# First layer: half of the out-projection woven into latent attention, three modulation vectors moved to neighbourhood attention

## The chip, the core and the metric

The kernel runs on one core of a Trainium2 chip. TensorE (PE) multiplies, VectorE (DVE) and ScalarE (ACT) do the elementwise work, GpSimd (POOL) has small tasks and a DMA queue of its own, and SyncE (SP) issues nearly all DMAs. The metric is device time in microseconds of one launch, the median of 3 runs; lower is better.

## The reference, cut to what matters

Two layers of a diffusion trunk over 512 latent tokens and 256 context tokens of width 1024. Each layer makes six modulation vectors for each of two streams, three parallel heads, one out-projection over their concatenation, and an MLP:

```python
mx, mc = _modulation(c, w_mod[i], b_mod[i]), _modulation(c_ctx[None], w_mod[i], b_mod[i])  # silu(cond) @ w + b, split in 6
px = _adaln(x, g_norm1[i], mx[0], mx[1]) @ w_in[i]                 # the same for context: pc
o_na  = _na_latent(...)      # 2-D neighbourhood attention, 4 heads of 64
o_mla = _mla_latent(...)     # latent attention, 8 heads
o_hy  = _hyena(...)          # order-2 Hyena, 256 channels
mix = concatenate([o_hy, merge(o_na), merge(o_mla)]) @ w_out[i]    # rows: 256 + 256 + 512
x = x + mx[2] * mix
x = x + mx[5] * _sqrelu_mlp(_adaln(x, g_norm2[i], mx[3], mx[4]), ...)
```

In the last layer only the latent stream is carried on (512 columns); in the first layer both streams are (768).

## The kernel before, in words

All activations lie feature-major: a tile is 128 features by 768 tokens (512 latent, 256 context). Most products run as three float32r matmuls on high and low parts (`wblock` loads 512 KB of weights, ACT makes the high part, DVE the low part). A product over 768 columns is a pair of matmuls of 512 and 256 columns.

One layer runs in this order: input projections; neighbourhood attention (`na_attend`) woven with the Hyena convolution (`hyena`, the name `conv`); latent attention (`mla_attend`); out-projection; MLP. `weave` takes generators with rates and steps each of them by its rate once a round, so the rates set the order in which work is traced. The framework lays out each engine's program from that order when the kernel is built; where nothing pins it, it may put an instruction ahead of one traced earlier if its inputs and a buffer are there (the first three blocks of `w_out` are loaded long before the out-projection is traced).

**Neighbourhood attention, first layer.** `na_attend` makes 16 rounds: in a round it scores unit u, writes the output of unit u-4 and transposes unit u-2; 8 units are latent, 4 context only. `hyena` has 14 steps at rate 1.4: 4 transposes, then for each of two orders two forward transforms (16 PE instructions each, then eight DVE operations that make `z`), and inverse transforms that need all of `z`. PSUM has 2 double banks ("mm") and 4 single banks ("b") here. The three buffers of the tag `raw` serve all weight blocks.

**Latent attention, first layer.** `mla_attend` makes 52 rounds for 48 units, in four groups of 12: 8 units over all 768 keys and then 4 that see 256 context keys only. In the first two of those four rounds the next two heads are turned (`heads_in`, 12 transposes a head). PSUM is 3 mm and 2 b banks. Woven into it at rate 0.2 each are `modulation` for vectors 2 and 4 (loads by SP; 32 matmuls of 32 x 256 a vector, which run four at a time in column groups) and `modulation_rows` for vector 3 (loads by SP, two DVE multiply-and-reduce operations for each of 8 blocks, and a SiLU over `cond_rows`).

**Out-projection.** In the last layer, `out_first` weaves the first half (contraction blocks 0 to 3: Hyena and neighbourhood outputs `mh`, `ml`) into latent attention, adds it to the residual `xT` through the gate, and only blocks 4 to 7 follow. In the first layer all 8 blocks follow latent attention: 8 output blocks x 8 contraction blocks x 3 x (512, 256) matmuls at L1341, while `fill` steps `modulation_rows` for (0,5) and the six vectors of layer 1 (L191) on DVE, one step an output block. `fill` goes on in the MLP.

Of the kernel before, what the change touches and what calls it, by code (L numbers as in the profile page):

```python
# [16 lines left out]
ALU = mybir.AluOpType  # L17
# [6 lines left out]
DEPTH = 2  # L24
# [17 lines left out]
def kernel(ctx, tc, A, dbg=None, stop=None):  # L42
    nc = tc.nc
    pe, act, dve, pool, sp = nc.tensor, nc.scalar, nc.vector, nc.gpsimd, nc.sync

# [93 lines left out]

    def mod_weights(l, v, k, p, bufs):  # L140
        w = p([128, 1024], tag="wm", bufs=bufs)
        sp.dma_start(w, A["w_mod"][l, k * 128:(k + 1) * 128, v * 1024:(v + 1) * 1024])
# [147 lines left out]
    H1 = 0.3  # L290
    OF = 1.0
    NSB, NPT = 3, 4
# [741 lines left out]

    def out_weights(j, half):

        return wblock(A["w_outh"][j, half])

    def out_first(l, xT, mh, ml, streams):

        for j in range(4):
            w = out_weights(j, 0)
            for e in range(2):
                t = b_tile()
                for k in range(4):
                    ws, xs = [x[:, e * 512 + k * 128:e * 512 + (k + 1) * 128] for x in w], [x[:, k] for x in (mh, ml)]
                    for i, (wx, mx) in enumerate(((0, 0), (0, 1), (1, 0))):
                        for a, b in streams:
                            pe.matmul(t[:, a:b], ws[wx], xs[mx][:, a:b], start=(k == 0 and i == 0),  # L1049
                                      stop=(k == 3 and i == 2))  # L1050
                    if k % 2:
                        yield
                add_gated(t, xT, 2 * j + e, l, 2, streams)
                yield

    def mlp(l, xT, hh, hl, rstd, streams, p, tail, fill=iter(())):
# [10 lines left out]
        def ff1(c):  # L1067
# [3 lines left out]
            for j in range(4):  # L1071
# [125 lines left out]
    for l in range(DEPTH):  # L1197
# [14 lines left out]
        if l:  # L1212
            squares, sums = mla_in(l, uh, ul, cqh, cql, ssq, sc, fill, late)
            sc.close()
            gp.close()
            xp.close()
# [63 lines left out]
        if not last:  # L1280
            hyena_out(1, y, mh, ml)
        weave((na_attend(l, na, nb, mh, ml, sc), 1.0), (conv, (1.4, 1.4)[l]))
        hyena_out(0, y, mh, ml)
        sc.close()
        hs.close()
        bp.close()
        yp.close()
# [9 lines left out]
        psum_banks(3)  # L1297
        if last:
            xp = Pool(f"x{l + 1}", "right")
            xT, acc = xp([128, KD, nt]), xp([128, nt])  # L1300
            sp.dma_start(xT, xd)
            weave((mla_attend(l, qrs, qk0, qkd[l], vd[l], mh2, ml2, sc), 1.0),
                  (out_first(l, xT, mh, ml, streams), OF))
        else:
            wmp = Pool("wm_rest")
            weave((mla_attend(l, qrs, qk0, qkd[l], vd[l], mh2, ml2, sc), 1.0),
                  (chain(*[modulation(0, v, wmp) for v in (2, 4)]), 0.2),
                  (modulation_rows([(0, 3)], cond_rows(wmp), wmp), 0.2))
            wmp.close()
        sc.close()  # L1310
# [4 lines left out]

        if not last:
            xp = Pool(f"x{l + 1}", "right")
            xT, acc = xp([128, KD, nt]), xp([128, nt])
            sp.dma_start(xT, A["xT"])
        gp = Pool(f"g{l}", "right")  # L1320
# [5 lines left out]
        for m in range(KD):  # L1326
            ks = range(8)
            if last:
# [4 lines left out]
            else:  # L1333
                w = wblock(A["w_out"][l, m])
            t = mm_tile()
# [12 lines left out]
            sumsq(acc, xT, m, nt, xp)  # L1348
            next(fill, None)
        split(hh[:, :, nt:nt + 2], hl[:, :, nt:nt + 2], mods[:, l, 3])  # L1350
# [10 lines left out]
        else:  # L1361
            def tail(m):
                sp.dma_start(xd[:, m], xT[:, m, 0:S])
                sumsq(acc, xT, m, nt, xp)
# [74 lines left out]
def _layout(inp):  # L1439
# [64 lines left out]
    a["w_in_v"] = blocks(np.concatenate([w[:, :, 1280:1536], w[:, :, 1920:]], 2), 8, 288)[:, 0, 0]  # L1504
    a["w_out"] = blocks(g["w_out"][:DEPTH - 1], 8, 128)[:, :, 0]
    a["w_outh"] = g["w_out"][-1].reshape(2, 4, 128, 4, 2, 128).transpose(3, 0, 2, 4, 1, 5).reshape(4, 2, 128, 8, 128)
    a["w_ff1"] = blocks(g["w_ff1"], 8, 128)[:, :, 0]
# [25 lines left out]
```

## Time and profile before

| | us |
|---|---|
| median of 3 runs | 1818.92 (1817.44 to 1821.12) |
| the profiled execution | 1826.58 |
| its span, first to last instruction | 1824.7 |
| neighbourhood attention, first layer | 282.86 to 355.45 |
| latent attention, first layer | 355.45 to 504.01 |
| out-projection, first layer | 504.01 to 571.90 |
| latent attention, last layer | 1324.23 to 1440.51 |

The stage bounds are the starts of the first PE instruction that belongs to the next stage; a few instructions lie across a bound. An fp32 product appears as two PE instructions at the same line, an fp32 transpose or a float32r product as one. A PE instruction's duration includes the time to run through the array, in which the next one already enters; so what a row of them costs is read from starts, not durations. The granted TensorE clock is 1.00 at 2.4 GHz and 0.50 at 1.2 GHz; a value between is a mean over a stretch.

### The profile page before, as it was taken

The numbers are of one execution on the slowest core, as the hardware profiler recorded it, in microseconds if no ns is written. First come the engines' busy times: TensorE is split into PE (matmuls) and PEld (weight loads), VectorE is DVE, ScalarE is ACT, GpSimd is POOL, SyncE is SP. The second block draws the span as 40 slices with busy tenths as digits, with TensorE's granted clock in tenths as the row PEclk, the third lists the DMA queues.
The fourth block names the chain that finished last, engine by engine and source line by source line (L and its number), as shares of the span: only waits on it lengthen the run. The fifth ranks groups of instructions, "written<-read, shape, count | busy, mean of one in ns | idle before, by whom it ended". The sixth has DMA issues, their size and how long they took to land.

```text
span 1824.7 us, 26988 instructions
## 1 busy us (share of the span) xinstructions
PE 1750.7 (96%) x10794; PEld 1498.3 (82%) x10794; DVE 1226.0 (67%) x2247; ACT 754.5 (41%) x1262; POOL 89.6 (5%) x137
## 2 busy tenths in 40 slices
PE   5999988988999999999999999989999999999999
PEld 2788977766688888888888888879787799999997
DVE  5857777877668868677675457686887665555554
ACT  3624326756634413212222225645666653333331
POOL 1134200000000000000000000230000000000000
PEclk9999989999999999999999999899999999999999
DMA  9225423262243433333332122353041023332232
GB/s 345 69 74 169 137 96 119 100 214 96 72 182 108 149 126 116 138 116 122 132 116 70 58 73 90 109 195 118 24 171 45 33 89 96 96 93 93 93 93 81
DMA packets 73388, 206.11 MB, mean 113 GB/s; under 512 B 12556, under 2 KB 24605, under 8 KB 71856
## 3 DMA queue, kind: packets, MB, share of 16 engines
q1 hardware_dynamic: 71664, 199.15, 32.3%
q0 software_dynamic: 1600, 5.24, 0.8%
q8 instruction: 85, 1.39, 0.3%
q14 instruction: 39, 0.32, 0.1%
HBM read 182.35 MB, written 21.23 MB: 112 GB/s over the span
## 4 chain that ended last, share of the span: by engine, by line
PE 86%; DVE 6%; ACT 4%; DMA 2%; issue 2%; POOL 0%; SPq 0%; DVEq 0%; ACTq 0%; POOLq 0%
PE mm L273 54%; PE mm L1341 5%; PE b L1008 3%; PE mm L995 3%; PE mm L131 2%; PE mm L133 2%; PE mm L132 2%; PE b L387 2%; PE b L131 1%; PE b L150 1%; PE b L132 1%; PE b L133 1%; PE b L350 1%; PE b L1049 1%; PE b L758 1%
## 5 line engine op out<-in xcount | busy, mean ns | idle before, releaser
L273 PE MATMUL mm<-t,wh 128*128 128x512 f32 (+1 forms) x2496 | 493.8, 318 | 2.5 <-DVE t L1032 1.3
L136 ACT ACTIVATE wh<-wr 128x1024 fp32r<-128x1024 f32 (+2 forms) x176 | 185.2, 1053 | 592.2 <-PE mm L273 532.3
L273 PEld LDWEIGHTS mm<-t,wh 128*128 128x128 f32 x2496 | 371.9, 189 | 39.4 <-issue 1.9
L273 PE MATMUL mm<-t,wl 128*128 128x512 f32 (+1 forms) x1248 | 297.1, 316 | 0.0
L137 DVE TENSOR_TENSOR wl<-wr,wh 128x1024 fp32r<-128x1024 f32 (+2 forms) x176 | 213.9, 1216 | 30.7 <-ACT wh L136 27.4
L273 PE MATMUL mm<-al,wh 128*128 128x512 f32 (+1 forms) x768 | 233.7, 359 | 0.0
L273 PE MATMUL mm<-ah,wl 128*128 128x512 f32 (+1 forms) x768 | 232.3, 356 | 0.0
L273 PE MATMUL mm<-ah,wh 128*128 128x512 f32 (+1 forms) x768 | 231.0, 355 | 0.0
L1032 DVE SCALAR_TENSOR_TENSOR t<-mm,mods,t 128x512 f32<-128x512 f32 x216 | 136.3, 659 | 140.4 <-PE mm L273 133.4
L273 PEld LDWEIGHTS mm<-t,wl 128*128 128x128 f32 x1248 | 193.7, 189 | 16.0 <-DVE wl L137 0.2
L273 PEld LDWEIGHTS mm<-ah,wl 128*128 128x128 f32 x768 | 127.7, 188 | 22.4
L273 PEld LDWEIGHTS mm<-ah,wh 128*128 128x128 f32 x768 | 126.9, 188 | 23.4
L273 PEld LDWEIGHTS mm<-al,wh 128*128 128x128 f32 x768 | 126.3, 188 | 20.0
L191 DVE SCALAR_TENSOR_TENSOR wmp<-wm,t 128x1024 f32<-128x1024 f32 x64 | 78.4, 1225 | 70.7 <-DMA wm<-in_w_modr_dram 70.7
L425 DVE TENSOR_REDUCE mmx<-mm 128x1 f32<-128x768 f32 (+1 forms) x80 | 67.5, 846 | 25.2 <-PE mm L133 24.5
L136 ACT ACTIVATE ah<-relu 128x768 fp32r<-128x768 f32 (+1 forms) x64 | 47.3, 739 | 86.9 <-DVE relu L1095 86.8
L430 ACT ACTIVATE msb<-mm,mmx,qrs 128x768 f32<-128x768 f32 (+1 forms) x80 | 72.1, 902 | 25.0 <-DVE mmx L427 21.3
L1085 DVE TENSOR_SCALAR bb<-mm,cols 128x2 f32<-128x2 f32 x64 | 14.0, 219 | 97.2 <-PE mm L273 97.0
L996 ACT ACTIVATE mpt<-mm 128x768 f32<-128x768 f32 (+1 forms) x80 | 57.5, 724 | 50.7 <-PE mm L995 50.6
L191 DVE SCALAR_TENSOR_TENSOR wm<-wm,t 128x1024 f32<-128x1024 f32 x64 | 78.1, 1220 | 0.2
L137 DVE TENSOR_TENSOR al<-relu,ah 128x768 fp32r<-128x768 f32 (+1 forms) x64 | 52.6, 823 | 36.2 <-ACT ah L136 36.1
L1341 PE MATMUL mm<-t,wh 128*128 128x512 f32 x320 | 75.2, 348 | 0.0
(294 smaller groups left out, 2864.6 us busy)
## 6 DMA issues: line engine op xcount, KB each, us to landing
wr<-in_w_ff_dram SPq DMA_DIRECT2D x128, 512.0 KB, 3.5
wm<-in_w_modr_dram SPq DMA_DIRECT2D x64, 512.0 KB, 4.4
wm<-in_w_mod_dram SPq DMA_DIRECT2D x32, 512.0 KB, 8.2
wr<-in_w_in_t_dram SPq DMA_DIRECT2D x18, 512.0 KB, 4.4
qk<-qk_spill SPq DMA_DIRECT2D x9, 576.0 KB, 5.2
qk_spill<-upk SPq DMA_DIRECT2D x12, 384.0 KB, 3.0
kx<-kk POOLq DMA_DIRECT2D x16, 256.0 KB, 2.4
wr<-in_w_in_qk_dram SPq DMA_DIRECT2D x8, 512.0 KB, 4.5
```

Of the source, the lines that this page charges most:

```text
L131: pe.matmul(out, sh, mh, start=start, stop=False)
L132: pe.matmul(out, sh, ml, start=False, stop=False)
L133: pe.matmul(out, sl, mh, start=False, stop=stop)
L136: act.activation(hi, src, AF.Copy)
L137: dve.tensor_sub(lo, src, r32(hi))
L191: dve.scalar_tensor_tensor(w if s else junk, w, 1.0, cr[:, s], ALU.mult, ALU.mult, accum_out=mods[:, l, v, k, s:s + 1])
L273: pe.matmul(out_[:, po:po + b - a], wk[wx], mk[mx][:, a:b], start=(k == 0 and i == 0), stop=(k == nk - 1 and i == 2))
L425: dve.tensor_reduce(mx, src, AX.X, ALU.max, negate=True)
L430: act.activation(sb[:, h, :n], src[:, h, :n], AF.Exp, bias=mx[:, h:h + 1], scale=1.0 if scale is None else scale[:, h:h + 1], accum_out=sm ...
L996: act.activation(pt[:, 0:nkt, qt * 128:(qt + 1) * 128], tt[:, :nkt * 128].rearrange("p (c q) -> p c q", q=128), AF.Copy)
L1032: dve.scalar_tensor_tensor(xT[:, m, a:b], t[:, a:b], mods[:, l, v, m, s:s + 1], xT[:, m, a:b], ALU.mult, ALU.add)
L1341: pe.matmul(t[:, a:b], ws[wx], half[mx][:, k % 4, a:b], start=(k == ks[0] and i == 0), stop=(k == 7 and i == 2))
```

## The change

In the first layer only (the last layer's code is rewritten but issues the same work):

- `out_first` is woven into `mla_attend` at rate 0.62 (32 steps), one b bank and one product a stream (512, then 256 columns). `xT` (3 MB) is loaded at the start of latent attention instead of its end. The loop after it keeps blocks 4 to 7.
- Vectors 2, 3 and 4 are made by `modulation` in the neighbourhood stage at rate 1.0: 5 steps a vector, 4 with a group of eight matmuls, one that copies, transposes and adds. The 24 loads of 512 KB are issued by POOL, in turn into `raw` buffers (3) and a new pool `wm_mid` (2 buffers).
- While that weave is traced, PE's order is pinned around the modulation's matmuls: each group of eight comes behind every PE instruction traced before it and ahead of all traced after it.
- `modulation_rows` for vector 3, its SiLU and its 16 DVE operations leave latent attention. The eight `fill` steps of the out-projection go: four now run in the first part of the MLP, four in its last.

```diff
+        def issue(self, r):
+            ins = r.ins
+            if self.on:
+                for prev in self.since if self.inside else []:
+                    self.after(ins, prev)
+                if self.last is not None:
+                    self.after(ins, self.last)
+                if self.inside:
+                    self.since, self.last = [], ins
+                else:
+                    self.since.append(ins)
+            return r
...
     def modulation(l, v, p, bufs=3, ws=None):
-        out = b_tile()
+        out, wk = b_tile(), []
         for k in range(KD):
-            w = ws[k] if ws else mod_weights(l, v, k, p, bufs)
-            for j in range(4):
-                pe.matmul(out[32 * j:32 * j + 32, 0:256], cst[:, k, :], w[:, j * 256:(j + 1) * 256],
-                          start=(k == 0), stop=(k == KD - 1), tile_position=(0, 32 * j))
+            if ws:
+                wk.append(ws[k])
+            elif k % 2:
+                wk.append(mod_weights(l, v, k, p, bufs, pool))
+            else:
+                wk.append(raw_tile())
+                pool.dma_start(wk[k], A["w_mod"][l, k * 128:(k + 1) * 128, v * 1024:(v + 1) * 1024])
             if k % 2:
+                with pe:
+                    for i in (k - 1, k):
+                        for j in range(4):
+                            pe.matmul(out[32 * j:32 * j + 32, 0:256], cst[:, i, :], wk[i][:, j * 256:(j + 1) * 256],
+                                      start=(i == 0), stop=(i == KD - 1), tile_position=(0, 32 * j))
                 yield
...
-    OF = 1.0
+    OF = 0.62
...
     def out_first(l, xT, mh, ml, streams):
         for j in range(4):
-            w = out_weights(j, 0)
+            w = out_weights(l, j, 0)
             for e in range(2):
-                t = b_tile()
-                for k in range(4):
...
+                for s, a, b in STREAM[:len(streams)]:
+                    t = b_tile()
+                    for k in range(4):
+                        ws = [x[:, e * 512 + k * 128:e * 512 + (k + 1) * 128] for x in w]
+                        for i, (wx, mx) in enumerate(((0, 0), (0, 1), (1, 0))):
+                            pe.matmul(t[:, 0:b - a], ws[wx], (mh, ml)[mx][:, k, a:b], start=(k == 0 and i == 0),
                                       stop=(k == 3 and i == 2))
+                        if k % 2 and s == 0:
+                            yield
+                    m = 2 * j + e
+                    dve.scalar_tensor_tensor(xT[:, m, a:b], t[:, 0:b - a], mods[:, l, 2, m, s:s + 1], xT[:, m, a:b],
+                                             ALU.mult, ALU.add)
+                    yield
...
-                for _ in range(FR if c else 0):
+                for _ in range(FR):
                     next(fill, None)
...
+        if not last:
+            wmp = Pool("wm_mid", "right")
+            mid = chain(*[modulation(0, v, wmp, 2) for v in (2, 3, 4)])
...
+            pe.order(True)
+            weave((na_attend(l, na, nb, mh, ml, sc), 1.0), (conv, 1.4),
+                  (mid, 1.0))
+            pe.order(False)
...
+        xp = Pool(f"x{l + 1}", "right")
+        xT = xp([128, KD, nt])
+        sp.dma_start(xT, xd if last else A["xT"])
+        weave((mla_attend(l, qrs, qk0, qkd[l], vd[l], mh2, ml2, sc), 1.0),
+              (out_first(l, xT, mh, ml, streams), (OF, 1.0)[l]))
...
         for m in range(KD):
-            ks = range(8)
-            if last:
-                ks = range(4, 8)
-                if m % 2 == 0:
-                    w2 = out_weights(m // 2, 1)
-                w = [x[:, m % 2 * 512:] for x in w2]
-            else:
-                w = wblock(A["w_out"][l, m])
+            ks = range(4, 8)
+            if m % 2 == 0:
+                w2 = out_weights(l, m // 2, 1)
+            w = [x[:, m % 2 * 512:] for x in w2]
...
-            next(fill, None)
```

## Rows read from the trace of the kernel before

**Rows 1.** The page: busy time of each engine, and the chain by engine.
```profile
PE 1750.7 (96%) x10794; PEld 1498.3 (82%) x10794; DVE 1226.0 (67%) x2247; ACT 754.5 (41%) x1262; POOL 89.6 (5%) x137
PE 86%; DVE 6%; ACT 4%; DMA 2%; issue 2%; POOL 0%; SPq 0%; DVEq 0%; ACTq 0%; POOLq 0%
```
**Rows 2.** Busy time by stage; length, engines with instruction counts, clock, DMA.
```profile
core 0: us, PE busy (x) PEld busy (x) DVE busy (x) ACT busy (x) POOL busy (x), PEclk, DMA share, GB/s
282.86:355.45 72.59, 64.67 (x505) 52.16 (x504) 59.70 (x125) 52.09 (x132) 0.00 (x0) 0.98 0.31 105
355.45:504.01 148.56, 134.92 (x911) 94.47 (x911) 108.94 (x261) 96.09 (x179) 0.00 (x0) 0.97 0.40 138
504.01:571.90 67.89, 67.89 (x392) 59.35 (x391) 52.90 (x85) 24.18 (x33) 0.00 (x0) 1.00 0.46 163
1324.23:1440.51 116.28, 116.26 (x753) 90.94 (x751) 83.57 (x167) 75.93 (x126) 0.00 (x0) 1.00 0.23 83
```
**Rows 3.** PE in order of time, latent attention of the last layer: start, length, line.
```profile
1374.88 0.82 PE L995 MATMUL mm<-ident,msb 128*128 128x128 f32 x6
1375.63 1.08 PE L1008 MATMUL b<-mpt,t 128*64 128x256 f32 x6
...
1377.44 0.29 PE L131 MATMUL mm<-kh,qh 96*128 96x256 f32 x1
1377.56 0.28 PE L132 MATMUL mm<-kl,qh 96*128 96x256 f32 x1
...
1377.89 2.37 PE L1008 MATMUL b<-mpt,t 128*64 128x256 f32 x18
1380.19 0.87 PE L995 MATMUL mm<-ident,msb 128*128 128x128 f32 x6
```
**Rows 4.** PE in order of time, the modulation's matmuls at the start.
```profile
44.49 3.23 PE L150 MATMUL b<-wm,cst 128*32 128x256 f32 x56
```
**Rows 5.** Groups of latent attention, first layer: count, busy us, mean ns, idle before.
```profile
L1008 PE MATMUL b<-mpt,t 128*64 128x256 f32 x218 | 36.1, 392 | 0.6 <-ACT mpt L996 0.5
L995 PE MATMUL mm<-ident,msb 128*128 128x128 f32 x224 | 35.6, 291 | 9.8 <-ACT msb L430 3.9 <-DVE msb L438 2.4 <-DVE ql L959 1.9
L191 DVE SCALAR_TENSOR_TENSOR wmp<-wm,t 128x1024 f32<-128x1024 f32 x8 | 9.8, 1220 | 4.0 <-DMA wm<-in_w_modr_dram 4.0
L171 ACT ACTIVATE t<-t 128x2048 f32<-128x2048 f32 x1 | 1.9, 1914 | 0.0
```
**Rows 6.** Stretches of latent attention, first layer, columns as in the second group.
```profile
401.00:425.79 24.79, 22.00 (x135) 14.60 (x133) 18.37 (x44) 14.02 (x29) 0.00 (x0) 1.00 0.41 135
425.79:440.75 14.96, 12.42 (x82) 9.19 (x80) 10.45 (x28) 8.65 (x17) 0.00 (x0) 0.89 0.34 114
440.75:461.51 20.76, 20.76 (x140) 14.75 (x140) 14.64 (x38) 14.78 (x29) 0.00 (x0) 1.00 0.17 52
```
**Rows 7.** Stretches of neighbourhood attention, first layer, columns as in the second group.
```profile
282.86:300.00 17.14, 11.76 (x93) 9.88 (x93) 12.50 (x33) 15.04 (x38) 0.00 (x0) 0.90 0.78 251
300.00:320.00 20.00, 17.55 (x145) 13.94 (x145) 19.26 (x32) 13.31 (x32) 0.00 (x0) 1.00 0.15 53
```
**Rows 8.** Groups of neighbourhood attention, first layer: two of the DVE operations behind `z`.
```profile
L744 DVE TENSOR_TENSOR tax<-usx,kkx 128x1024 f32<-128x1024 f32 x4 | 4.9, 1220 | 0.0
L746 DVE TENSOR_TENSOR tax<-tax 128x512 f32<-128x512 f32 x4 | 2.8, 688 | 0.0
```
**Rows 9.** DMAs: SP's loads at L142, then POOL's stores at L396.
```profile
DMA to landing us min/median/max: 3.4/8.2/12.3
L396 POOL DMA_DIRECT2D kx<-kk x16: 539/542/710, 72.9 to 154.1; - x16
DMA to landing us min/median/max: 2.3/2.5/3.0
```
**Rows 10.** Out-projection, first layer: the DVE groups of L191.
```profile
L191 DVE SCALAR_TENSOR_TENSOR wmp<-wm,t 128x1024 f32<-128x1024 f32 x11 | 13.5, 1225 | 0.6 <-DMA wm<-in_w_modr_dram 0.6
L191 DVE SCALAR_TENSOR_TENSOR wm<-wm,t 128x1024 f32<-128x1024 f32 x10 | 12.2, 1225 | 0.1
```

More of the change, by code (lines that the diff above doesn't have):

```diff
@@ L43, with __init__, after, matmul @@
     nc = tc.nc
-    pe, act, dve, pool, sp = nc.tensor, nc.scalar, nc.vector, nc.gpsimd, nc.sync
+    act, dve, pool, sp = nc.scalar, nc.vector, nc.gpsimd, nc.sync
+    class Ordered:
+        def __init__(self):
+            self.on, self.inside, self.last, self.since = False, False, None, []
+        def after(self, ins, prev):
+            tc.add_manual_dep(ins, prev.name, mybir.DependencyInfo(
+                mybir.DependencyClass.NoSync, mybir.DependencyReason.DATA))
+        def issue(self, r):
[10 more added lines that the diff above has]
+            return r
+        def matmul(self, *a, **k):
+            return self.issue(nc.tensor.matmul(*a, **k))
+        def transpose(self, *a, **k):
+            return self.issue(nc.tensor.transpose(*a, **k))
+        def order(self, on):
+            self.on, self.last, self.since = on, None, []
+        def __enter__(self):
+            self.inside = True
+        def __exit__(self, *_):
+            self.inside = False
+    pe = Ordered()
     class Stop(Exception):
@@ L137, in split, with mod_weights @@
         dve.tensor_sub(lo, src, r32(hi))
-    def mod_weights(l, v, k, p, bufs):
+    def mod_weights(l, v, k, p, bufs, queue=sp):
         w = p([128, 1024], tag="wm", bufs=bufs)
-        sp.dma_start(w, A["w_mod"][l, k * 128:(k + 1) * 128, v * 1024:(v + 1) * 1024])
+        queue.dma_start(w, A["w_mod"][l, k * 128:(k + 1) * 128, v * 1024:(v + 1) * 1024])
         return w
     def modulation(l, v, p, bufs=3, ws=None):
-        out = b_tile()
+        out, wk = b_tile(), []
         for k in range(KD):
-            w = ws[k] if ws else mod_weights(l, v, k, p, bufs)
-            for j in range(4):
-                pe.matmul(out[32 * j:32 * j + 32, 0:256], cst[:, k, :], w[:, j * 256:(j + 1) * 256],
-                          start=(k == 0), stop=(k == KD - 1), tile_position=(0, 32 * j))
-            if k % 2:
+            if ws:
[5 more added lines that the diff above has]
+                pool.dma_start(wk[k], A["w_mod"][l, k * 128:(k + 1) * 128, v * 1024:(v + 1) * 1024])
+            if k % 2:
+                with pe:
[3 more added lines that the diff above has]
+                                      start=(i == 0), stop=(i == KD - 1), tile_position=(0, 32 * j))
                 yield
@@ L1033, in add_gated, with out_weights @@
                                      ALU.mult, ALU.add)
-    def out_weights(j, half):
-        return wblock(A["w_outh"][j, half])
+    def out_weights(l, j, half):
+        return wblock(A["w_outh"][l, j, half])
     def out_first(l, xT, mh, ml, streams):
         for j in range(4):
-            w = out_weights(j, 0)
+            w = out_weights(l, j, 0)
             for e in range(2):
-                t = b_tile()
-                for k in range(4):
[L1046 to L1049, printed above, removed]
-                                      stop=(k == 3 and i == 2))
[L1051 to L1054, printed above, removed]
+                for s, a, b in STREAM[:len(streams)]:
[4 more added lines that the diff above has]
+                            pe.matmul(t[:, 0:b - a], ws[wx], (mh, ml)[mx][:, k, a:b], start=(k == 0 and i == 0),
+                                      stop=(k == 3 and i == 2))
+                        if k % 2 and s == 0:
[4 more added lines that the diff above has]
+                    yield
     def mlp(l, xT, hh, hl, rstd, streams, p, tail, fill=iter(())):
@@ L1215 @@
             gp.close()
+            ap_.close()
             xp.close()
@@ L1281 @@
             hyena_out(1, y, mh, ml)
-        weave((na_attend(l, na, nb, mh, ml, sc), 1.0), (conv, (1.4, 1.4)[l]))
+        if last:
+            weave((na_attend(l, na, nb, mh, ml, sc), 1.0), (conv, 1.4))
+        else:
+            pe.order(True)
+            weave((na_attend(l, na, nb, mh, ml, sc), 1.0), (conv, 1.4),
+                  (mid, 1.0))
+            pe.order(False)
         hyena_out(0, y, mh, ml)
@@ L1285 @@
         hs.close()
+        if not last:
+            wmp.close()
         bp.close()
@@ L1297 @@
         psum_banks(3)
-        if last:
[L1299 to L1303, printed above, removed]
-        else:
[L1305 to L1309, printed above, removed]
+        xp = Pool(f"x{l + 1}", "right")
[3 more added lines that the diff above has]
+              (out_first(l, xT, mh, ml, streams), (OF, 1.0)[l]))
         sc.close()
@@ L1314 @@
             return finish_all()
[L1316 to L1319, printed above, removed]
+        ap_ = Pool(f"acc{l + 1}", "right")
+        acc = ap_([128, nt])
         gp = Pool(f"g{l}", "right")
@@ L1326 @@
         for m in range(KD):
-            ks = range(8)
-            if last:
-                ks = range(4, 8)
-                if m % 2 == 0:
-                    w2 = out_weights(m // 2, 1)
-                w = [x[:, m % 2 * 512:] for x in w2]
-            else:
-                w = wblock(A["w_out"][l, m])
+            ks = range(4, 8)
+            if m % 2 == 0:
+                w2 = out_weights(l, m // 2, 1)
+            w = [x[:, m % 2 * 512:] for x in w2]
             t = mm_tile()
@@ L1363, in tail @@
                 sp.dma_start(xd[:, m], xT[:, m, 0:S])
-                sumsq(acc, xT, m, nt, xp)
+                sumsq(acc, xT, m, nt, ap_)
                 for s, a, b, o in ((0, 0, S, 0), (1, S, NT, S + 2)):
@@ L1504, in _layout @@
     a["w_in_v"] = blocks(np.concatenate([w[:, :, 1280:1536], w[:, :, 1920:]], 2), 8, 288)[:, 0, 0]
-    a["w_out"] = blocks(g["w_out"][:DEPTH - 1], 8, 128)[:, :, 0]
-    a["w_outh"] = g["w_out"][-1].reshape(2, 4, 128, 4, 2, 128).transpose(3, 0, 2, 4, 1, 5).reshape(4, 2, 128, 8, 128)
+    a["w_outh"] = g["w_out"].reshape(DEPTH, 2, 4, 128, 4, 2, 128).transpose(0, 4, 1, 3, 5, 2, 6).reshape(
+        DEPTH, 4, 2, 128, 8, 128)
     a["w_ff1"] = blocks(g["w_ff1"], 8, 128)[:, :, 0]
```

2 lines of the change are left out of this document (1 added, 1 removed).

## Prediction

> **What bounds the kernel now.** I read the page's totals first, then its chain, then a table of busy time by stage, and only then single groups. The totals and the chain say PE: 96% busy, 86% of the chain [rows 1]. That average hides three stages with different limits [rows 2]. The first layer's out-projection is PE alone: busy for all of its 67.89 us, and DVE and ACT have time left. Latent attention before it shows PE busy for 134.92 of 148.56 us, neighbourhood attention for 64.67 of 72.59 us.
>
> A busy PE is not yet a full one: a single matmul counts as busy while it runs through the array, though another could have entered. So I count instructions and price them by the distance of starts where PE is dense [rows 3]: six transposes of L995 take 0.75 us, 0.125 each; eighteen instructions of L1008 take 2.30 us, 0.128 each; a float32r matmul of 256 columns 0.12 us. In the out-projection 384 matmuls, 192 pairs, fill 67.89 us less eight strays of 0.128: 0.348 a pair, so 0.228 for the 512 columns [rows 2, 3]. The modulation's instructions cost 3.23/56 = 0.058 each [rows 4].
>
> The first layer's latent attention by these prices: 224 x 0.125 + 218 x 0.128 [rows 5], by the code 96 x 0.228 and 144 x 0.12 for scores and 96 x 0.125 to turn heads: 28.0 + 27.9 + 21.9 + 17.3 + 12.0 = 107 us. The two modulation vectors add 128 instructions x 0.058 = 7.4. So 114.5 of 148.56 us are PE's work, and 34 us are gaps, seen or covered. The last layer is the measure of the method: 192 x 0.125 + 192 x 0.128 + 96 x 0.228 + 96 x 0.12 + 80 x 0.125, and 96 x 0.228 for the half out-projection already woven there: 114 of 116.28 us, 98% full at clock 1.00 [rows 2]. The same weave therefore can fill PE.
>
> The Trainium skill (Trainium Kernel Development and Optimization, Performance Expectations) says that matmul busy time is a bad measure because matmuls are pipelined. Rows 2 agree: 134.92 us busy against 114.5 us counted. By the busy column the 33.4 us that move would find 13.6 us of room in latent attention; that is the second rival below.
>
> **Out-projection.** It loses half of its 192 pairs: 96 x 0.348 = **-33.4 us**. What was beside it: DVE was busy 52.90 us, of which the 21 operations of L191 that ran there took 13.5 + 12.2 [rows 2, 10]; they leave. Some 27 us at most remain, less four of eight weight splits, in a stage of 33.5 us. DVE thus stays under PE, by a smaller margin. The second half needs blocks 4 to 7, of which the last comes from the end of latent attention; the last layer starts in the same way with no PE gap. The weights are the same bytes. I bound this term by -34 and -30 (some gaps where DVE is late). The eight `fill` steps go to the MLP's first and last parts, where the other parts already carry four such steps; I price them at nothing, and at up to 1 us if DVE is late at the seam.
>
> **Latent attention.** Added: 96 pairs, 33.4 us of PE, four weight splits, 16 gated adds. Removed: 7.4 us of modulation matmuls, sixteen L191 operations of 1.22 us on DVE, and the SiLU of 1.9 us [rows 5]. That SiLU sits with two table loads in front of the first softmax; the 3.9 us wait of L995 on ACT [rows 5] goes with it. PE's work becomes 107 + 33.4 = 140.4 us. Lower bound of the stage: as full as the last layer, 140.4/0.98 = 143, so -5.5. Upper bound: the stretches over all keys are dense already once DVE is rid of L191 (20.76 us in the third group, 24.79 in the second) [rows 6], so there the woven work costs its full price; only the context stretches (14.96 us with PE busy 12.42, at clock 0.89) [rows 6] can hide it. They are 16 of 52 rounds and take 16 x 0.62 = 10 of the 32 steps, 10.4 us. Then 33.4 - 10.4 = 23 is paid; 3.9 (SiLU), 4 + 4 (the first two groups without L191) and two thirds of 7.4 come off: +6. A PE that no longer idles would also keep its clock: 0.89 over 14.96 us is a loss of 1.6 us. The mean of the ends is about 0; I take **-1 us**, as the last layer speaks for the lower end. The load of `xT` moves here from the end of the stage and lies ahead of the values (1.5 MB) on SP's queue; the first gated add comes in round 5, some 14 us in, and the last layer runs the same order.
>
> **Neighbourhood attention.** Added: 3 x 64 instructions x 0.058 = 11.1 us, and six transposes of 0.12, together 11.8 us of PE; ACT gets three small copies, DVE a few operations on a handful of columns. PE idles for 5.4 us until 300 and for 2.5 us until 320 [rows 7], 7.9 in the stage [rows 2]. The twelve groups lie over the first 14 of 16 rounds, and a round is 72.6/16 = 4.5 us, so seven or eight fall into these two stretches, 0.93 us each: I let them fill the second gap, 2.45 us, and 2.9 of the first, together 5.3. In the second DVE is busy 19.26 of 20 us: there it sets the pace and PE's extra work is free. That gives 11.8 - 5.3 = **+6.5 us**. The lower bound is 0 (all fits beside DVE). The upper: nothing fits, +11.8, and the pinned order adds stalls. A group stands behind everything traced before it; in the round of the second forward transform that is also the inverse transform, which waits for `z`: two operations of 1.22, two of 0.68 and four of 0.69 on DVE, 6.6 us [rows 8]. Today PE goes on with attention meanwhile. There are two such places, so +13 at most: +25 in all. Each falls on a round whose modulation step has no group, so PE has two rounds of attention to fill it with; I charge none of it in the value. The running sum holds one b bank of four for four rounds; this too lies within the upper end.
>
> The loads: 24 x 512 KB through POOL's queue, whose engine is otherwise idle here (0.00 busy) [rows 2]. Five buffers hold two and a half groups, so a load has about two rounds, 9 us, from its buffer's release to its use. SP's loads of this same size took 8.2 us in the median and 3.4 to 12.3; POOL's stores of 256 KB are issued in 0.54 us and land in 2.5 [rows 9]. Five blocks fit into the buffers ahead of the stage; the other 19, 10 MB, add 137 GB/s over 72.6 us to the 105 there now: 242, about the 251 that the first stretch already reaches [rows 2, 7]. I price the loads at nothing beyond the 6.5; what waits behind a late one is all of PE, by the pinned order.
>
> The Trainium skill (SBUF — State Buffer, SBUF: two separate sides) says that GpSimd cannot write the descriptors of its DMAs while DVE runs a two-port operation. No run here shows it: the stores above ran before this stage. By that rule each load would land later by up to one such operation; it raises the chance of the last rival a little.
>
> **Sum.** -33.4 - 1 + 6.5 = -28 us. Against the profiled execution, 1826.58 - 28 = 1798.6; that execution stands 7.7 us above the median shown, so the predicted median is 1818.92 - 28 = **1791**.
>
> **Rivals.** *All fits*: neighbourhood attention hides its 11.8 us and latent attention reaches 143: -33.4 - 5.5 = -39, 1780. For it the last layer's density, against it PE's thin idle time after 320. *Latent attention is already full*: the 33.4 us only move, and 7.4 leave: -33.4 + 33.4 - 7.4 + 6.5 = -1, 1818, no change. For it PE's busy column, against it the count. *The pinned order stalls*: neighbourhood attention +20 with latent attention at +4: -9, 1810. For it the two waits on `z` and the lost bank; against it that DVE has other work meanwhile. *Slower: the loads starve PE.* If POOL's queue served one load after another at 8.2 us each, the 19 that are not there at the start would take 156 us instead of 72.6: +83, and -34 elsewhere: +49, 1868. It is slower than before from (72.6 + 34)/19 = 5.6 us a load on. Against it: POOL's stores land in 3.0 us at the most, and SP's loads overlap.
>
> **How the numbers follow.** Forecast 0.62, all fits 0.12, stalls 0.12, already full 0.06, starved 0.06, else 0.02. The forecast's own range is 1783 to 1801 (both bounds of each term, half used). To leave out no more than two in ten I reach into the two neighbours: 1778 to 1810. A change under 0.2%, 3.6 us, cannot be told from none here. Faster by more: 0.62 + 0.12 + 0.11 + 0.01 = 0.86; within: 0.06; slower: 0.08.
>
> **What would show it.** L1341 in the first layer: half the count in 33 to 35 us. Latent attention 143 to 152 us with clock 1.00 throughout and no wait of L995 on ACT near its start. Neighbourhood attention 73 to 84 us; a wait of L150 on its loads of more than 1 us a group would speak for starvation, a wait of L758 or L769 on `z` of several us for the pinned order. The forecast is wrong if latent attention grows by over 8 us or neighbourhood attention by over 15.

## The result, and the profile after

| | us |
|---|---|
| changed kernel, median of 4 runs | 1792.4 (1790.59 to 1801.18) |
| kernel before, median of 4 runs beside it | 1820.0 (1817.44 to 1822.04) |
| ratio | 0.9852, 95% interval 0.983 to 0.9874 |
| profiled execution of the changed kernel, its span | 1788.8 |

The change takes 27.6 us off; the forecast was 28, with 1791 as the time. The sum came out by luck: neighbourhood attention cost 7 us more than its term and the out-projection gave 2.2 less, while latent attention gave 4.5 more and a gain of 2.7 was in no term.

All PE instructions of the changed kernel go through one helper and carry its lines (L69, L72), so they are told apart by their tiles. The page's totals and its chain, which answer to [rows 1] (the chain's shares add up to 78% only, so its 75% does not compare with the 86% of before):

```profile
PE 1730.5 (97%) x10860; PEld 1489.3 (83%) x10860; DVE 1220.3 (68%) x2232; ACT 752.2 (42%) x1260; POOL 101.1 (6%) x161
PE 75%; DVE 2%; ACT 1%; issue 0%; DMA 0%; ACTq 0%; DVEq 0%; SPq 0%
```

The three stages (columns as in [rows 2]): neighbourhood attention, latent attention, out-projection. The end of the last line lies one matmul behind the MLP's first one, which starts at 544.62; counted as before, the out-projection is 36.67 us.

```profile
279.00:364.84 85.84, 76.99 (x703) 57.22 (x703) 62.09 (x130) 54.47 (x134) 10.38 (x19) 0.98 0.55 192
364.84:507.95 143.11, 141.60 (x960) 113.08 (x958) 105.10 (x243) 94.63 (x177) 0.00 (x0) 1.00 0.24 88
507.95:544.86 36.91, 36.91 (x212) 31.61 (x212) 28.84 (x48) 21.36 (x30) 0.00 (x0) 1.00 0.34 115
```

Against [rows 2]: 85.84 - 72.59 = +13.25; 143.11 - 148.56 = -5.45; 36.67 - 67.89 = -31.22; together -23.4 us. PE in neighbourhood attention is busy 12.3 us longer and idle for 8.85 us, where it was 7.92 before. Of the 8.85, 1.8 are new waits for loads; so of the old gaps 0.9 us at most were filled. In latent attention it is idle for 1.51 us, where it was 13.64.

PE in neighbourhood attention, in order of time (start, length, tiles, idle before): first the start of the stage, then its end. The groups of the modulation are those that read `cst`.

```profile
280.58 0.64 PE L69 MATMUL b<-wr,cst 128*32 128x256 f32 x8
281.03 0.61 PE L69 MATMUL b<-wm,cst 128*32 128x256 f32 x8
281.58 0.98 PE L69 MATMUL mm<-t,t 64*128 64x256 f32 x12
...
284.80 0.98 PE L69 MATMUL mm<-t,t 64*128 64x256 f32 x12 [0.57 <-ACT nsb L596]
289.08 1.94 PE L72 MATMUL b<-ident,nsb 128*128 128x128 f32 x8 [3.31 <-DVE nsb L485]
...
357.92 0.64 PE L69 MATMUL b<-wr,cst 128*32 128x256 f32 x8
358.80 0.64 PE L69 MATMUL b<-wm,cst 128*32 128x256 f32 x8 [0.24 <-DMA wm<-in_w_mod_dram]
...
360.54 0.64 PE L69 MATMUL b<-wr,cst 128*32 128x256 f32 x8
362.73 0.64 PE L69 MATMUL b<-wm,cst 128*32 128x256 f32 x8 [1.55 <-DMA wm<-in_w_mod_dram]
```

A group takes 281.58 - 280.58 = 1.00 us of PE. Two of them run ahead of the 3.31 us in which PE waits for the first softmax, none in it. The last two wait for their loads, 1.8 us, with PE behind them.

A second trace of the same kernel tells what belongs to one execution. Its stages are 86.46, 143.15 and 36.67 us (the first has clock 0.96 in place of 0.98). But the first matmul of the input projections started at 50.40 us in one execution and at 57.85 in the other, and the 30 us around the end of the first layer had clock 0.89 and 0.83:

```profile
50.40 1.27 PE L69 MATMUL mm<-t,wh 128*128 128x512 f32 x5
```
```profile
57.85 0.93 PE L69 MATMUL mm<-t,wh 128*128 128x512 f32 x3
```
```profile
1110.00:1140.00 30.00, 27.07 (x177) 26.38 (x176) 20.55 (x57) 22.51 (x49) 3.02 (x9) 0.89 0.24 76
```
```profile
1117.00:1147.00 30.00, 27.07 (x172) 26.74 (x171) 19.37 (x54) 21.45 (x44) 2.16 (x6) 0.83 0.18 53
```

The profiled execution of before had 54.12 us there and clock 0.77 at the layer's end, so of the 35.9 us between the two spans some 7 (3.7 at the start, 0.12 x 30 = 3.6 at the layer's end) are the executions'. What remains, 28.6, agrees with the medians' 27.6.

### The profile page after: what moved, and what is told of

It is laid out like the page before. It is cut to its first block, busy times and chain, and to the rows that moved or that the text cites. A ratio compares the mean times of both kernels' runs of the same rounds, so it can differ in the third digit from the quotient of the medians.

```text
span 1788.8 us, 27117 instructions
## 1 busy us (share of the span) xinstructions
PE 1730.5 (97%) x10860; PEld 1489.3 (83%) x10860; DVE 1220.3 (68%) x2232; ACT 752.2 (42%) x1260; POOL 101.1 (6%) x161
## 4 chain that ended last, share of the span: by engine, by line
PE 75%; DVE 2%; ACT 1%; issue 0%; DMA 0%; ACTq 0%; DVEq 0%; SPq 0%
PE mm L69 61%; PE b L69 10%; PE mm L72 4%; PE b L72 1%; ACT t L289 0%; ACT t L175 0%; DVE nmx L472 0%; DMA qk_spill<-upk 0%; DVE usx L790 0%; DVE tax L791 0%; ACT cz L746 0%; DVE usx L792 0%; DVE wl L176 0%; ACT t L690 0%; DVE t L674 0%
## 5 line engine op out<-in xcount | busy, mean ns | idle before, releaser
L69 PE MATMUL mm<-t,wh 128*128 128x258 f32 (+2 forms) x2688 | 541.5, 320 | 1.8 <-DVE t L176 0.6
L69 PEld LDWEIGHTS mm<-t,wh 128*128 128x128 f32 x2688 | 403.1, 189 | 45.2 <-issue 3.1
L69 PE MATMUL mm<-t,wl 128*128 128x512 f32 (+1 forms) x1344 | 326.6, 319 | 0.0
L69 PE MATMUL mm<-ah,wh 128*128 128x512 f32 (+1 forms) x768 | 231.4, 356 | 0.0
L69 PE MATMUL mm<-al,wh 128*128 128x512 f32 (+1 forms) x768 | 230.7, 355 | 0.0
L69 PE MATMUL mm<-ah,wl 128*128 128x512 f32 (+1 forms) x768 | 230.4, 355 | 0.0
L69 PEld LDWEIGHTS mm<-t,wl 128*128 128x128 f32 x1344 | 209.6, 189 | 19.4 <-DVE wl L176 0.2
L69 PEld LDWEIGHTS mm<-ah,wh 128*128 128x128 f32 x768 | 126.2, 188 | 22.6
L69 PEld LDWEIGHTS mm<-al,wh 128*128 128x128 f32 x768 | 126.9, 188 | 20.4
L69 PEld LDWEIGHTS mm<-ah,wl 128*128 128x128 f32 x768 | 125.8, 187 | 21.4
L238 DVE SCALAR_TENSOR_TENSOR wmp<-wm,t 128x1024 f32<-128x1024 f32 x56 | 68.5, 1224 | 67.1 <-DMA wm<-in_w_modr_dram 67.1
L69 PE MATMUL b<-wh,t 128*128 128x256 f32 (+1 forms) x416 | 93.3, 306 | 4.3 <-ACT hu L662 3.5
L69 PEld LDWEIGHTS b<-wh,t 128*128 128x128 f32 x416 | 72.6, 203 | 6.1 <-ACT hu L662 4.0
L176 DVE TENSOR_TENSOR al<-relu,ah 128x768 fp32r<-128x768 f32 (+1 forms) x64 | 52.5, 823 | 33.5 <-ACT ah L175 33.4
```

The lines of the kernel that those rows point to most:

```text
L69: return self.issue(nc.tensor.matmul(*a, **k))
L176: dve.tensor_sub(lo, src, r32(hi))
L238: dve.scalar_tensor_tensor(w if s else junk, w, 1.0, cr[:, s], ALU.mult, ALU.mult, accum_out=mods[:, l, v, k, s:s + 1])
```

## The experiments

All times are medians; ratios are to the kernel before on the same chip (95%). Stage lengths are from each kernel's trace; the out-projection ends where the MLP's first matmul starts.

| kernel | us | ratio | neighbourhood | latent | out-proj. |
|---|---|---|---|---|---|
| changed, again | 1794.9 | 0.984 to 0.988 | 86.46 | 143.15 | 36.67 |
| no pinned order | 1801.3 | 0.987 to 0.992 | 91.19 | 143.79 | 36.67 |
| modulation alone | 1816.8 | 0.995 to 0.998 | 86.83 | 130.11 | 69.14 |
| one load | 1793.9 | 0.983 to 0.988 | 84.80 | 142.81 | 36.67 |
| half rounds | 1798.3 | 0.985 to 0.991 | 90.90 | 143.14 | 36.67 |
| early at 0.4 | 1793.1 | 0.980 to 0.988 | 80.82 | 143.01 | 36.67 |
| SP's queue | 1794.2 | 0.981 to 0.987 | 85.84 | 143.72 | 36.67 |
| before, no rows | 1810.6 | 0.990 to 0.995 | 72.60 | 133.61 | 69.14 |
| rate 1.0 | 1796.4 | 0.982 to 0.987 | 85.75 | 146.84 | 35.22 |
| placed, 4 early | 1793.0 | 0.982 to 0.986 | 83.14 | 142.96 | 36.67 |
| placed, 3 early | 1793.5 | 0.983 to 0.986 | 85.16 | 142.90 | 36.67 |
| placed, 5 early | 1797.0 | 0.984 to 0.988 | 88.15 | 142.88 | 36.67 |

**Modulation alone.** In the first layer only `mla_attend` is woven, and the out-projection keeps 8 blocks:

```diff
-              (out_first(l, xT, mh, ml, streams), (OF, 1.0)[l]))
+              *([(out_first(l, xT, mh, ml, streams), 1.0)] if last else []))
```

> The changed kernel, but the first layer's out-projection is not woven: all 8 blocks follow latent attention, as in the kernel before; the three vectors stay in neighbourhood attention. Theory (latent attention has gaps that the woven half fills): without it latent attention is 130 to 138 us against 143.11, so the woven half costs 5 to 13 of its 33.4 us there; out-projection 67 to 68 us; the time 1812 to 1820 us. Rival (the gain of latent attention comes from the vectors that left it, and the woven half is paid in full): latent attention 108 to 114 us, the time 1790 to 1796 us.

Latent attention, out-projection (with one matmul too many at its end), and the first 32 us of latent attention:

```profile
367.78:497.89 130.11, 121.99 (x780) 88.51 (x779) 91.39 (x225) 91.35 (x174) 0.00 (x0) 0.98 0.22 85
497.89:567.26 69.37, 69.37 (x392) 59.61 (x392) 38.41 (x60) 24.53 (x33) 0.00 (x0) 1.00 0.30 99
367.78:400.00 32.22, 26.76 (x165) 21.45 (x164) 23.02 (x49) 21.58 (x35) 0.00 (x0) 0.91 0.58 233
```

The theory holds for latent attention and the time, at its upper edge; the out-projection of 69.14 us, expected at 67 to 68, is taken up in the last section. From 148.56 to 130.11, 18.45 us, come from what left the stage; the woven half then costs 13.0 us. With it PE has 180 instructions more (x960 against x780, 12 of the 192 fall behind the bound), 32.0 us by the forecast's price, yet its busy time grows by 19.6 only. So of the 19.0 us that were not paid, 6.6 went into idle time (8.12 to 1.51) and 12.4 into time that had counted as busy. Part of the 12.4 is the clock: without the woven half it is 0.91 over the first 32.22 us, a loss of up to 2.9 us; with it, 1.00. PE's first wait in this stage, with no SiLU in it:

```profile
380.16 1.50 PE L72 MATMUL mm<-ident,msb 128*128 128x128 f32 x6 [3.65 <-DVE msb L485]
```

It is nearly as long as the 3.9 us of [rows 5], and 1.17 us in the changed kernel (376.69, the same instruction). But before, a group of the modulation's matmuls stood in the same gap. From the end of the scores to that instruction it is 4.48 us before (363.46 to 367.94) and 3.65 us here (376.51 to 380.16): about 0.8 us of it were the SiLU's, the rest is the latency of the first softmax. In the changed kernel it is 3.29 us (373.40 to 376.69), and woven matmuls fill 2.1 of them.

**Before, no rows.** The second generator of the weave goes:

```diff
-                  (modulation_rows([(0, 3)], cond_rows(wmp), wmp), 0.2))
```

> The kernel before, but vector 3 of the first layer is not computed (set to zero): its 16 operations of 1.22 us on DVE, its loads and its SiLU leave latent attention; the matmuls of vectors 2 and 4 stay. Without them and without the matmuls that stage was 130.1 us against 148.56, so 18.5 us are to be shared. Theory (my terms: 3.9 for the SiLU, 8 for DVE's rows, 5 to 7 for the matmuls): the stage is 135 to 138 us. Rival (the matmuls and their waits cost nearly all): 144 us or more. Other rival (DVE and ACT cost nearly all): 130 to 132 us.

```profile
352.75:486.37 133.62, 130.23 (x911) 91.75 (x911) 91.94 (x228) 91.92 (x176) 0.00 (x0) 0.99 0.29 101
```

Between the theory and the second rival: DVE's rows and the SiLU cost 14.9 us, the 7.4 us of matmuls (the rest of the 18.45) 3.5. DVE is freed of 17 us (108.94 to 91.94), and the stage gains nearly all of it, though DVE was busy for 73% only. The likely reason is that its rows stood between the softmaxes for which PE waited; how much of the 14.9 is theirs and how much the SiLU's (ACT is freed of 4.2 us) no run separates.

**Rate 1.0.** `OF = 0.62` becomes `OF = 1.0`.

> The changed kernel, but the half out-projection is woven into latent attention at rate 1.0 in place of 0.62, as in the last layer: its 32 steps are done after 32 of the 52 rounds. Theory (the woven matmuls fill the gaps of the rounds that they stand in, so they must be spread over all rounds): the later rounds keep their gaps, latent attention is 146 to 149 us against 143.11, the time 3 to 6 us above the changed kernel's. Rival (the gaps that the work fills lie at the start of the stage): 142 to 144 us, no difference.

```profile
367.50:514.34 146.84, 143.86 (x972) 114.86 (x971) 107.03 (x245) 96.43 (x178) 0.00 (x0) 1.00 0.24 90
```

The theory holds: 3.73 us longer, PE idle for 2.98 us. The out-projection is 1.45 us shorter, as no woven product is left over at its start, so 2.3 us remain. That lies within the ratio's interval; the trace alone shows it.

**No pinned order.** `pe.order(True)` goes.

> The changed kernel, but PE's order isn't pinned around the modulation's matmuls. Theory (PE pays the twelve groups in full wherever they stand, 12 x 0.93 us, because the gaps of the stage are waits for results that nothing else can fill): neighbourhood attention stays at 84 to 87 us (85.84 in the changed kernel), the time within 2 us of it. Rival (the pinned order stalls PE): the stage falls to 78 to 80 us, which is what I predicted without stalls, and the time by about 6 us.

```profile
288.67 0.63 PE L69 MATMUL b<-wr,cst 128*32 128x256 f32 x6
295.42 1.08 PE L69 MATMUL b<-wm,cst 128*32 128x256 f32 x8 [6.12 <-DMA wm<-in_w_mod_dram]
```

Both wrong, and the rival has the wrong sign. At the same clock (0.96) the stage is 4.7 us longer than the changed kernel's: the framework puts the third and fourth group before their blocks have landed, and PE stands for 6.12 us behind them. The pinned order does not stall here; it keeps the groups behind work that covers their loads. Whether a free order fills the gaps once the blocks have landed was not run.

**One load.** Every matmul reads the block loaded first:

```diff
-            elif k % 2:
-                wk.append(mod_weights(l, v, k, p, bufs, pool))
-            else:
-                wk.append(raw_tile())
-                pool.dma_start(wk[k], A["w_mod"][l, k * 128:(k + 1) * 128, v * 1024:(v + 1) * 1024])
+            else:
+                if not one:
+                    one.append(mod_weights(l, v, k, p, 1, pool))
+                wk.append(one[0])
```

> The changed kernel, but all 192 modulation matmuls read one loaded block: 23 of the 24 loads are left out, the instructions of PE are the same (the vectors' values are not the reference's). Theory (the stage pays PE's work, the loads only the last wait of 1.8 us): neighbourhood attention 83.5 to 84.5 us, the time 2 us under the changed kernel's. Rival (the loads slow the stage: they share the DMA engines with its other loads in the first 17 us, at 350 GB/s): the stage 78 to 80 us, the time 6 to 8 us less.

```profile
282.46:367.26 84.80, 76.87 (x704) 57.50 (x703) 62.05 (x132) 54.35 (x134) 0.00 (x0) 0.96 0.20 65
```

The theory holds: DMA falls from 192 to 65 GB/s, and the stage loses 86.46 - 84.80 = 1.66 us at the same clock, which is the two waits at its end (0.19 and 1.50 in the second trace of the changed kernel). The rest is PE's: it is idle for 7.93 us here, as long as the 7.92 us before, and busy for 12.2 us more than before. The time is not lower; in this trace the stages from the first projection matmul to neighbourhood attention took 230.65 us against 228.60.

**SP's queue.** Both `pool` arguments of the loads become `sp`.

> The changed kernel, but the 24 modulation loads are issued by SP's queue in place of POOL's. Theory (the queue that issues is not what costs, PE's work is): a load now stands in SP's program between others that wait for buffers, so some land later; neighbourhood attention 86 to 89 us, the time 0 to 4 us above the changed kernel's. Rival (POOL's queue is needed: on SP the modulation's loads and the weight preloads hold each other up): the stage over 92 us, the time 6 us or more above.

Theory right in kind (the stage stays under its 86 to 89 us): it is 85.84 us with either queue. In its trace the stages from the first projection matmul to neighbourhood attention took 231.1 us against 228.6, and the medians do not differ.

**Half rounds.** `na_attend` yields once more, ahead of the transposes, and the modulation's step stands there:

```diff
+            if l < DEPTH - 1:
+                yield
             if LV <= u < n + LV:
                 turn(u - LV)
             yield
...
-            weave((na_attend(l, na, nb, mh, ml, sc), 1.0), (conv, 1.4),
-                  (mid, 1.0))
+            weave((na_attend(l, na, nb, mh, ml, sc), 1.0), (mid, 0.5), (conv, 0.7))
```

> The changed kernel, but each round of neighbourhood attention is traced in two halves, scores and output first, then the transposes; the modulation's step stands between the two, the convolution's step after. Theory (a group is free only where PE waits for softmax just then): two or three groups fall into the waits of the first 10 us, the stage is 82 to 84 us, the time 2 to 4 us less. Rival (the place within a round does not matter, since DVE and ACT set the length of the waits): 85 to 86 us, no difference.

```profile
315.68 0.66 PE L72 MATMUL b<-ident,nsb 128*128 128x128 f32 x4 [0.69 <-ACT npt L609]
319.47 2.08 PE L69 MATMUL b<-zx,t 128*128 128x256 f32 x4 [3.14 <-DVE zx L797]
```

The edit did not do what the expectation says: at rate 0.5 the modulation's step fires in the second half of each round, so a group still stands behind the transposes (PE waits for the first softmax as before, 2.87 us). What moved is the convolution, whose steps now come behind the group. The stage is 4.4 us longer at the same clock, and PE waits 3.14 us for `z` against 1.57 in the changed kernel. Whether a group between scores and transposes would be free stays open. That moving the convolution costs 4 us is shown; which part of that is the order and which the split of its steps is not, as the edit changes both.

**Early and placed groups.** PE waits three times (2.68, 1.10, 3.46 us) in the stage before, where queries and keys are projected. The first try weaves the modulation in there at rate 0.4 (`stage` and `part` end its share with the stage); the others name the rounds (round: steps):

```diff
+            pe.order(True)
+            weave((stage(na_qk(l, hh, hl, na, sc)), 1.0), (hyena(l, 1, y, sc), 0.8), (part(mid), 0.4))
+            pe.order(False)
...
+                    for _ in range({8: 2, 10: 1, 12: 1}.get(r, 0)):
+                        next(g)
```

> The changed kernel, but the modulation starts earlier: its first five steps (four groups and the finish of vector 2) are woven at rate 0.4, with PE's order pinned, into the stage before, where neighbourhood attention's queries and keys are projected and PE waits three times (2.68, 1.10 and 3.46 us); the other ten follow as before. Theory (a group is free only where PE waits just then): the groups near these waits are hidden, neighbourhood attention loses its last groups and their waits on loads (1.8 us) and is 78 to 81 us, the stage before grows by 0 to 2 us, the time is 2 to 5 us under the changed kernel's. Rival (each group is paid in full wherever it stands): what neighbourhood attention loses the stage before gains, 4 us, and only the 1.8 us of waits go, or nothing.

> The changed kernel, with four groups of the modulation in the stage before, as in the earlier try, but placed: two in the round ahead of the longest wait (3.46 us for the convolution's product), one two rounds later, one in the last. Theory (early groups cost there because the running sum holds a b bank while two waits for banks follow, and are free in front of the longest wait): the stage before grows by 1 to 2.5 us, neighbourhood attention falls from 85.8 to 80 to 82 us, the time is 2 to 4 us under the changed kernel's. Rival (paid in full wherever they stand, as in the earlier try): 4 us here, 5 less there, the time within 1.5 us of the changed kernel's.

> As the placed version with four early groups, and the finish of vector 2 (copy, two transposes, add) also in the stage before; so the steps left in neighbourhood attention are the ten of the first early try. Theory (a group costs where it makes a later one late: with ten steps no group stands between the last inverse transforms, where the eleven-step version waited 2.56 us for their input): the stage before as long as in the changed kernel (within 1 us), neighbourhood attention 80.5 to 82 us, the time 3 to 5 us under the changed kernel's, thus 1788 to 1792 beside a kernel before of 1821. Rival (what the placed version saved in one stage comes back in the other): the two stages together no shorter than in the placed version, 1793 or more.

The round ahead of the longest wait, in the changed kernel, then in the version with four placed groups, which stand at 259.30 to 261.2 (two) and later:

```profile
256.81 1.89 PE L69 MATMUL b<-uc,t 128*128 128x256 f32 x8
...
265.35 1.19 PE L69 MATMUL b<-t,zc 128*128 128x128 f32 x4 [3.46 <-DVE zc L795]
```
```profile
259.75 0.61 PE L69 MATMUL b<-wm,cst 128*32 128x256 f32 x8
260.19 0.61 PE L69 MATMUL b<-wr,cst 128*32 128x256 f32 x8
260.62 0.61 PE L69 MATMUL b<-wm,cst 128*32 128x256 f32 x8
...
265.48 0.68 PE L69 MATMUL b<-t,zc 128*128 128x128 f32 x4 [0.85 <-DVE zc L795]
```

From the first projection matmul to neighbourhood attention the changed kernel takes 228.6 us, rate 0.4 takes 232.55 and the placed version 228.68. So at rate 0.4 the rival holds (+3.95 here, -5.0 there): behind its first group a matmul waits 2.15 us for ACT, a wait that the changed kernel does not have, and its second comes after the wait it might have filled. Placed, the four groups together cost this stage nothing. Two stand ahead of the longest wait, which falls from 3.46 to 0.85 us; the other two, of about 1 us each, stand ahead of no wait, and PE's granted clock can account for most of them. From 262 to 270 us, in the changed kernel and in the placed version:

```profile
262.00:270.00 8.00, 4.65 (x27) 4.68 (x28) 5.93 (x19) 0.64 (x2) 0.00 (x0) 0.79 0.00 0
262.00:270.00 8.00, 7.15 (x62) 6.94 (x61) 6.84 (x20) 1.52 (x5) 0.63 (x2) 1.00 0.67 251
```

A clock of 1.00 in place of 0.79 over 8 us is worth up to 1.7 us (over the whole 62 us it is 0.92 and 0.94). Neighbourhood attention gains 2.7 us of the placing, less than the theory's 4 or more, since its remaining groups now meet a wait of 2.56 us for `z` near its end. The version with three groups missed its theory too: it gains 1.3 us at equal clock (85.16 against 86.46), where 3 to 5 were expected. Its expectation:

> As the last one without the group in the last round: three groups in the stage before, twelve steps left for neighbourhood attention. Theory: the stage before grows by 0 to 1.5 us, neighbourhood attention falls to 81 to 83 us, the time 2 to 4 us under the changed kernel's. Rival (paid in full): 3 us here, 3 to 4 less there, no difference.

The version with five steps was to avoid that wait, and did, but its second group in neighbourhood attention stands ahead of the first wait, and its block was asked for at 280.98 us, when the stage's own loads had just filled the DMA engines. It landed after 12.3 us, with PE behind it; at 88.15 us the stage is the longest of the four, and the rival holds:

```profile
286.13 0.64 PE L69 MATMUL b<-wr,cst 128*32 128x256 f32 x8
293.31 1.08 PE L69 MATMUL b<-wm,cst 128*32 128x256 f32 x8 [6.54 <-DMA wm<-in_w_mod_dram]
```

None of these is faster than the changed kernel by more than the intervals: the best, 1793.0 against 1794.9 with four placed groups, is 0.1%. The changed kernel's own second run had this expectation, and its theory holds:

> The changed kernel itself, for a time on the same chip as the next two and for a second trace of it. Theory (the first 50 us and the falls of PE's clock at layer ends differ from one execution to the next, the stages between do not): neighbourhood attention 85 to 86.5 us, latent attention 142.5 to 143.5, out-projection 36.5 to 37.5; the time 1790 to 1796 us. Rival (the traced stage lengths are those of one execution): one of the three stages differs by over 2 us.

## Why the prediction was right or wrong

**Out-projection, -33.4: right in size, -31.2.** The 96 pairs take 33.9 us. Most of the missing 2.2 us, 1.4, is the tail of latent attention that lies behind the first instruction of this stage (2.75 us of it, 1.33 before); by as much the next term looks better than it is. Another 0.6 is a slower pace of PE: twelve pairs take 4.24 us, 0.353 each, where they took 4.16, 0.347 (last section). DVE stays under PE, 28.84 of 36.91 us.

**Latent attention, -1: the stage reached its lower bound, -5.45.** The step that failed is the upper end: "only the context stretches can hide it", so 23 us of 33.4 paid. Measured: 13.0 of 32.0 paid, so 19.0 hidden, where the upper end had room for 10.4 in the context stretches. The stretches over all keys that showed PE busy without a break were not full; in them the woven work cost less than its price, as the count of the forecast's first part (107 us of work in the stage) said and its upper end then forgot. What left the stage gave 18.45 us; my terms for it were 3.9 + 8 + 4.9 = 16.8, near in sum, wrong in their shares: DVE's rows and the SiLU 14.9, the matmuls 3.5. The first wait belongs to the softmax for the most part; about 0.8 us of it was the SiLU's.

The Trainium skill (Trainium Kernel Development and Optimization, Performance Expectations) calls matmul busy time a bad measure. The traces agree: 180 added instructions raised PE's busy time by 19.6 us (121.99 to 141.60). The rival by that column, "already full", predicted 1818 and is out.

**Neighbourhood attention, +6.5: too little, +13.25.** The step that failed: "I let them fill the second gap, 2.45 us, and 2.9 of the first". The forecast's terms were 11.8 of work less 5.3 in gaps and nothing for loads. Measured: 12.3 of work, 0.9 of the old gaps filled (none with one load), 1.8 of waits for loads, so +13.25; the 85.84 us lie outside the 73 to 84 that were to show it. The rival "all fits" is out with that, though its half in latent attention came true. A gap here is a wait of PE's next instruction for DVE or ACT, and an instruction that is in order behind that one cannot use it. What filled a gap here were groups just ahead of the wait with nothing late behind them: two in the placed version took 2.6 us off a wait. The two groups ahead of the softmax in the changed kernel run while nothing else waits for PE, but the stage as a whole did not get their time back.

**Pinned order, charged none: right.** Without it the stage was 4.7 us longer. The one stall on `z` is 1.57 us. **Loads, charged none: short by 1.7 to 1.8.** They do not queue one behind the other: the two of a pair are issued 0.54 us apart and land after 4.2 and 5.4 us in the median. POOL's loads in the stage, into `raw` buffers and into `wm_mid`:

```profile
DMA to landing us min/median/max: 3.9/4.2/10.3
DMA to landing us min/median/max: 4.7/5.4/11.9
```

The long ones are those of the first 13.7 us, when the stage moves 339 GB/s. In the changed kernel PE is waiting for the softmax just then. The starvation rival is out; yet a single late load can hold PE: where a group was put ahead of one, PE stood 6.1 and 6.5 us.

The Trainium skill (SBUF — State Buffer, SBUF: two separate sides) has GpSimd blocked from writing descriptors while DVE runs two-port operations. Nothing here shows it: POOL's issues in the stage took 0.54 us each (0.74 once), and SP's queue gave the same 85.84 us. Whether any of DVE's operations in this stage is a two-port one, no trace tells.

**Not in the forecast: the MLP.** PE's instructions go through it 0.5% faster, 2.7 us over 540 us (last section). **The sum** -31.2 - 5.45 + 13.25 - 2.7 = -26.1 stands against -27.6 (interval -31 to -23). That forecast and result agree is luck: the 6.75 and 2.2 us by which two terms came out worse nearly cancel the 4.5 and 2.7 that came unforeseen.

## What to carry to other kernels

A stage whose PE counts as busy for 94% of it (121.99 of 130.11 us) may still take half of another stage's matmuls at 40% of their price; count instructions at their dense spacing, and spread the added work over all rounds. Gaps between dependent instructions are different: in these runs work filled them only where it stood directly ahead of the wait and its data had landed, so look at each gap's neighbours in program order instead of subtracting idle time. And what leaves a stage is worth what waited for it: 17 us of DVE work and a SiLU off the chain of softmaxes gave 15 us, 7.4 us of matmuls gave 3.5.

## Not expected of the hardware

The MLP of the first layer runs the same sequence of matmuls, yet PE starts more of them in 150 us at a granted clock of 1.00. Before, then changed:

```profile
700.00:850.00 150.00, 150.00 (x852) 131.01 (x851) 109.53 (x164) 38.49 (x48) 0.00 (x0) 1.00 0.35 123
```
```profile
673.00:823.00 150.00, 150.00 (x856) 131.15 (x855) 109.82 (x167) 38.83 (x48) 0.00 (x0) 1.00 0.36 126
```

From the MLP's first matmul to the 3048th behind it, it takes 540.0 us before and 537.3 in both traces of the changed kernel, so the pace belongs to the built kernel and not to one execution. Kernels with the whole out-projection in one piece (before, modulation alone, no rows) show 852, the changed kernel and the one with rate 1.0 show 856. The out-projection has a second such pair, the other way round: twelve pairs take 4.16 us in the kernel before and 4.24 us in each of the other 13 traces. In the kernel without rows, which still has all 192 pairs, it is 69.14 us in place of 67.89 (the line ends one matmul behind it):

```profile
486.37:555.74 69.37, 69.37 (x393) 59.63 (x393) 53.32 (x87) 24.42 (x33) 0.00 (x0) 1.00 0.50 177
```

DVE's work is not the reason: modulation alone has the same 69.14 us with DVE busy for 38.41 us. So a price per matmul read from one build of a kernel holds for another to 2% only. In the last layer's MLP, kernel before and after keep step to 0.01 us. The cause was not found.

How long the chip stays at half clock after a stretch with gaps differs between executions of one kernel (0.89 and 0.83 over the same 30 us), and so does the start, by up to 7 us; a difference of two profiled executions has to be taken stage by stage.
